# Norm roots on columns of sums, one scan for four groups, and layer norm applied on ScalarE, in a hybrid decoder step

## The chip, the cores and the metric

The kernel runs on 1 core of one Trainium2 chip. The metric is the device time of one execution in microseconds (us). The engines that matter are TensorE (PE; its weight loads are listed apart as PEld), VectorE (DVE), ScalarE (ACT), GpSimd (POOL), and SyncE (SP), whose queue issues nearly all DMA transfers. Each engine runs its own queue in order.

## The reference

One layer over 1088 tokens (1024 of a prompt, 64 of eight short continuations), width 1024: a norm, a projection into three parts of 512, an S5 state-space mixer on the first part, a chunked gating mixer on the other two, a norm on each mixer's output, an output projection, then norm, SwiGLU feed-forward and a final norm.

```python
def rmsnorm(x, g):
    r = lax.rsqrt(jnp.mean(xf * xf, axis=-1, keepdims=True) + EPS)
    return xf * r * g
def layer(x, h0r, h0i, l):
    p = rmsnorm(x, norm1[l]) @ w_in[l]
    o_s5, hr, hi = s5_mixer(p[..., :512], h0r, h0i, ...)   # complex diagonal scan, GELU, GLU
    o_cm, v_rows = chunk_mixer(p[..., 512:], ...)          # GELU, layernorm(v), tril(W_s) @ v, u * mixed
    mix = concatenate([rmsnorm(o_s5, g_s5[l]), rmsnorm(o_cm, g_cm[l])])
    x = x + mix @ w_out[l]
    return x + swiglu(rmsnorm(x, norm2[l]), w_gate[l], w_up[l], w_down[l])   # then rmsnorm(x, norm_f)
```

## The kernel before

Activations lie feature-major: 128 features on the partitions, tokens along the free axis. Tokens are taken in three chunks of 384, 384 and 320 up to the mixers' outputs (`CH`), and in four of 272 (`NH`) from the output projection on. Large products run as three single-pass matmuls on a high and a low part of each operand (`mm3`, lines 150 to 152); the parts are made by `split` (a copy on ScalarE at line 146, a subtraction on VectorE at line 147).

The stages stand in this order. **Head**, 0 to 72 us: tokens and `w_in` come in, norm1 sums squares, VectorE builds the S5 tables of powers, and TensorE makes `pu`, the S5 input; VectorE writes it to SBUF as `us`, scaled by the root `rB` (line 303). **S5 stage**, 72 to 236 us: eight passes of four groups each (`s5_a`, `s5_b`, `s5_c`) with a scan over 128 blocks, and beside them, on TensorE, the projections `pv` and `pu` of the gating mixer, its layer norm (`ln`) and its mixing (`cm_out`). **Mixers' norms, GLU (`pg`) and output projection (`po`)**, 236 to 360; **norm2 and the first operands of the feed-forward** (`x_prep`), 360 to 396; **feed-forward**, 396 to 1078; **final norm** (`finish`), 1078 to the end.

Norms need, for each token, a sum over features, which lie on partitions. `sum_sq` (line 164) multiplies a 128x128 matrix of ones with the squares, so the sum comes out on all 128 partitions at once, in PSUM as `ss`, as wide as the chunk. `rsqrt_bc` takes the root there on all of it: one activation on ScalarE (line 171), then three VectorE steps of refinement (172 to 174), each 128 x chunk. In chunk 0 of norm1 each of the eight blocks of squares goes to TensorE; in chunks 1 and 2 VectorE adds them first (`sqs`, line 195). The projection `pv` comes out token-major, so its scale must be a column: nine VectorE operations read the diagonal of `rB` into `r1c` (line 624).

The S5 pass scans four groups one after the other (line 559), each with its own decay as a constant along the row. Around each scan stand two half swaps by DMA (`Sw<-Ss`, `gw<-gt`), a correction written as `Hp`, the output matmuls `yb`, a GELU to `ys`, and a trip through DRAM (`ys_d`) to the GLU's operand `g`.

Who runs when is set at build time: the framework's scheduler sorts all instructions by a model of their times and freezes the order of each engine's queue; a few `issue_after` lines pin things. So an edit also moves instructions that it does not touch.

## Time and profile before

| | us |
|---|---|
| median of 3 runs | 1108.19 (1107.27 to 1110.16) |
| the profiled execution, whole | 1110.51 |
| its span in the trace | 1108.7 |
| PE busy | 1052.7 (95%) |
| DVE busy | 855.2 (77%) |
| ACT busy | 431.4 (39%) |
| POOL busy | 322.1 (29%) |

The shares are averages over stages that differ. In the feed-forward TensorE is busy nearly all the time and VectorE two thirds; in the head and the S5 stage both are nearly full and wait for each other. So each stage is read by itself: who is idle there, and what ended the idle time. [...]

### The profile page before, as it was taken

How to read it: one execution, taken by the hardware profiler on the slowest of the kernel's cores; microseconds unless marked ns; L12 is line 12 of the kernel's file. 1: busy time of each engine (PE TensorE's matmuls, PEld its weight loads, DVE VectorE, ACT ScalarE, POOL GpSimd, SP SyncE). 2: the span in 40 equal slices, each digit the busy share in tenths (PEclk: the TensorE clock that was granted, in tenths of full speed). 3: DMA queues.
4: the chain of work that ended last, by engine and by line, in shares of the span. 5: the costliest groups of instructions: out<-in, count | busy, mean ns of one | idle time of the engine just before them, and what ended most of it. 6: DMA issues, size and time to landing. Idle time of an engine off the chain costs nothing.

```text
span 1108.7 us, 20330 instructions
## 1 busy us (share of the span) xinstructions
PE 1052.7 (95%) x7966; PEld 1027.8 (93%) x7966; DVE 855.2 (77%) x1724; ACT 431.4 (39%) x810; POOL 322.1 (29%) x287
## 2 busy tenths in 40 slices
PE   7899999969999899999999999999998999999994
PEld 6799998869999789999999999999998999999994
DVE  7988999898988996666666666657668768757886
ACT  7314323477444443233233232232244324314561
POOL 5010350000000435425435334435333333223220
PEclk9999999989999899999999999999999999999998
DMA  8342335365233113223224223133256816514304
GB/s 278 106 139 54 95 106 150 83 193 163 97 103 107 45 57 128 74 90 131 74 74 129 85 82 128 58 109 117 69 174 223 303 39 202 185 35 150 118 16 161
DMA packets 81519, 131.19 MB, mean 118 GB/s; under 512 B 8976, under 2 KB 60048, under 8 KB 81296
## 3 DMA queue, kind: packets, MB, share of 16 engines
q1 hardware_dynamic: 81424, 129.91, 36.9%
q8 instruction: 62, 1.02, 0.4%
q14 instruction: 33, 0.27, 0.1%
HBM read 90.43 MB, written 34.24 MB: 112 GB/s over the span
## 4 chain that ended last, share of the span: by engine, by line
PE 69%; DVE 15%; DMA 8%; issue 3%; ACT 3%; POOL 1%; SPq 0%; DVEq 0%; POOLq 0%; ACTq 0%
PE u L151 12%; PE u L150 12%; PE u L152 12%; DMA h<-hid_d 4%; PE po L152 3%; PE po L151 3%; PE po L150 3%; PE ua L151 3%; PE ua L150 3%; PE ua L152 3%; PE pv L151 2%; PE pv L150 2%; PE pv L152 2%; PE ub L151 1%; PE ub L152 1%
## 5 line engine op out<-in xcount | busy, mean ns | idle before, releaser
L1052 POOL TENSOR_TENSOR tS<-q,q 128x512 f32<-128x512 f32 x22 | 29.5, 1342 | 247.0 <-DVE h L914 146.1
L150 PE MATMUL u<-xh,h 128*128 128x272 f32 x344 | 99.1, 288 | 0.0
L151 PE MATMUL u<-xl,h 128*128 128x272 f32 x344 | 99.0, 288 | 0.0
L152 PE MATMUL u<-xh,h 128*128 128x272 f32 x344 | 98.9, 288 | 0.0
L146 ACT ACTIVATE h<-q 128x512 fp32r<-128x512 f32 (+1 forms) x83 | 50.7, 614 | 81.9 <-PE u L151 59.3
L147 DVE TENSOR_TENSOR h<-q,h 128x512 fp32r<-128x512 f32 (+1 forms) x83 | 71.7, 865 | 4.1 <-ACT h L146 2.3
L150 PE MATMUL pu<-xh,cwr 128*128 128x384 f32 (+1 forms) x192 | 65.6, 346 | 6.2 <-DVE us L303 6.2
L1090 ACT ACTIVATE st<-st 128x272 f32<-128x272 f32 x88 | 37.8, 431 | 71.9 <-DVE st L1112 34.5
L152 PE MATMUL pu<-xh,cwr 128*128 128x384 f32 (+1 forms) x192 | 64.9, 341 | 0.0
L151 PEld LDWEIGHTS u<-xl,h 128*128 128x128 f32 x344 | 64.8, 189 | 0.0
L151 PE MATMUL pu<-xl,cwr 128*128 128x384 f32 (+1 forms) x192 | 64.7, 338 | 0.0
L150 PEld LDWEIGHTS u<-xh,h 128*128 128x128 f32 x344 | 64.7, 188 | 0.0
L152 PEld LDWEIGHTS u<-xh,h 128*128 128x128 f32 x344 | 64.6, 188 | 0.0
L1057 POOL TENSOR_TENSOR tS<-tS,q 128x512 f32<-128x512 f32 x22 | 30.4, 1381 | 114.7 <-DVE h L147 61.6
L146 ACT ACTIVATE fb<-q 128x512 fp32r<-128x512 f32 (+1 forms) x64 | 38.9, 609 | 57.2 <-PE u L151 38.9
L151 PE MATMUL u<-xl,fb 128*128 128x272 f32 x208 | 60.4, 290 | 0.6 <-DVE xl L147 0.6
L150 PE MATMUL u<-xh,fb 128*128 128x272 f32 x208 | 60.4, 290 | 0.0
L152 PE MATMUL u<-xh,fb 128*128 128x272 f32 x208 | 60.4, 290 | 0.0
L147 DVE TENSOR_TENSOR fb<-q,fb 128x512 fp32r<-128x512 f32 (+1 forms) x63 | 54.2, 864 | 3.7 <-ACT fb L146 2.8
L150 PE MATMUL po<-xh,cwr 128*128 128x272 f32 x192 | 56.3, 294 | 0.0
L1092 DVE TENSOR_TENSOR st<-st 128x272 f32<-128x272 f32 x88 | 54.5, 620 | 2.0
L151 PE MATMUL po<-xl,cwr 128*128 128x272 f32 x192 | 55.5, 289 | 0.0
(496 smaller groups left out, 4128.9 us busy)
## 6 DMA issues: line engine op xcount, KB each, us to landing
hid_d<-st SPq DMA_DIRECT2D x22, 952.0 KB, 4.2
...
```

The lines of the kernel that those rows point to most:

```text
L146: S.activation(hi, src, AF.Copy)
L147: return (eng or V).tensor_tensor(lo, src, hi.bitcast(F32), ALU.subtract)
L150: PE.matmul(p, wh, ah, start=start, stop=False, **kw)
L151: PE.matmul(p, wh, al, start=False, stop=False, **kw)
L152: return PE.matmul(p, wl, ah, start=False, stop=stop, **kw)
L1052: P.tensor_tensor(tS, a21, a22, ALU.add)
L1057: P.tensor_tensor(tS, tS, a11, ALU.subtract)
L1090: S.activation(dst, src, AF.Silu)
L1092: V.tensor_tensor(dst, dst, src, ALU.mult)
```

## The change

Sums of squares are made the other way round: `sum_cols` loads 128x128 squares as the weights and multiplies them with a single column of ones, so 128 tokens' sums come out as one column, 128x1, in PSUM (`cs`). A chunk has three such columns. The root is then taken on 128x3 numbers (`rsqrt_row`, tile `rcs`). TensorE spreads it: the root's column, repeated 128 times, is the weight matrix, and the identity moves, which gives the root along the free axis on all partitions (`rb`, PSUM). ScalarE copies it to SBUF, except in `finish`, where VectorE reads PSUM. The additions into `sqs` and the diagonal reads are gone; `pv`'s scale is the root's column itself. The identity is loaded ahead of the tokens.

The four scans become one over 128x512, with the decays in a table `mg` whose first column in each group is zero, so that a group starts afresh. ScalarE fills `mg` once a pass, into one buffer. Layer norm's last step goes from VectorE to ScalarE, with its bias made by a 128x1 operation on POOL.

```diff
-    def sum_sq(sq, n, p=None, first=True, last=True):
-        p = bank("ss", "sp")[:, :n] if p is None else p
-        LAST["sum"] = PE.matmul(p, ones, sq, start=first, stop=last)
+    def sum_cols(sqs, n, p=None, first=True, last=True):
+        p = bank("cs", "sp") if p is None else p
+        for i, sq in enumerate(sqs):
+            for j, (x, _) in enumerate(blocks(n)):
+                LAST["sum"] = PE.matmul(p[:, j:j + 1], sq[:, x:x + 128], ones[:, 0:1], start=first and i + j == 0,
+                                        stop=last and i == len(sqs) - 1, skip_group_check=True)
         return p
-    def rsqrt_bc(pl, p, n, scale):
+    def rsqrt_row(p, n, scale, out=None, tag="sp"):
+        r, a = (rcs[:, k, 3 * i:3 * i + len(bl)] for i in range(2))
+        LAST["rsqrt"] = S.activation(r, p, AF.Abs_reciprocal_sqrt, scale=scale, bias=epsc)
+        V.scalar_tensor_tensor(a, p, EPS / scale, r, op0=ALU.add, op1=ALU.mult)
+        V.scalar_tensor_tensor(a, a, -0.5 * scale, r, op0=ALU.mult, op1=ALU.mult)
+        V.scalar_tensor_tensor(r, a, 1.5, r, op0=ALU.add, op1=ALU.mult)
+        b = bank("rb", tag)[:, :n]
+        for j, (x, w) in enumerate(bl):
+            PE.matmul(b[:, x + 128 - w:x + 128], r[:, j:j + 1].to_broadcast([128, 128]), idn[:, 128 - w:128],
+                      start=True, stop=True)
+        if out is None:
+            return b, r
+        S.activation(out, b, AF.Copy)
+        return out, r
...
-            if c:
-                accum_sq(prep, sqs[:, :n], r[:, i, :], k == 0)
-            else:
-                N1["p"] = sum_sq(sq, n, N1.get("p"), k == 0, k == 7)
+            sq = tmp_sq(prep, n, "sq")
+            S.activation(sq, r[:, i, :], AF.Square)
+            N1[c] = sum_cols([sq], n, N1.get(c), k == 0, k == 7)
...
-        y = rsqrt_bc(prep, sum_sq(sqs[:, :n], n) if c else N1["p"], n, 1.0 / D)
-        V.tensor_copy(rB[:, n0:n0 + n], y)
+        R1[c] = rsqrt_row(N1[c], n, 1.0 / D, rB[:, n0:n0 + n], "s5")[1]
...
+        mg = mgs[pi % MG]
+        S.activation(mg[:, :, 1:128], mag8[:, gs].unsqueeze(2).to_broadcast([128, 4, 127]), AF.Copy)
...
-        V.tensor_tensor(rt, rt, Sw, ALU.add)
-        for g in range(4):
-            V.tensor_tensor_scan(gt[:, g, :], mag8[:, g0 + g:g0 + g + 1].to_broadcast([128, 128]), rt[:, g, :], 0.0,
-                                 ALU.mult, ALU.add)
+        V.tensor_tensor(Sw, rt, Sw, ALU.add)
+        V.tensor_tensor_scan(*(x.rearrange("p g c -> p (g c)") for x in (gt, mgs[pi % MG], Sw)), 0.0,
+                             ALU.mult, ALU.add)
...
-    for j in range(9):
-        V.scalar_tensor_tensor(jk, rB[:, tok(j)], 1.0, idn, op0=ALU.mult, op1=ALU.mult, accum_out=r1c[:, j:j + 1])
...
-        V.tensor_scalar(vj, vj, mv[:, j, 0:1], mv[:, j, 1:2], op0=ALU.subtract, op1=ALU.mult)
+        P.tensor_scalar(mv[:, j, 0:1], mv[:, j, 0:1], mv[:, j, 1:2], -1.0, op0=ALU.mult, op1=ALU.mult)
+        S.activation(vj, vj, AF.Identity, scale=mv[:, j, 1:2], bias=mv[:, j, 0:1])
...
-        rb = rsqrt_bc(cwp, sum_sq(sqo[:, n0:n0 + n], n), n, 1.0 / W)
+        rb, _ = rsqrt_row(sum_cols([sqo[:, n0:n0 + n]], n), n, 1.0 / W, row_tile(cwp, n))
...
-        p = sum_sq(ACC[c], NH, bank("ss", ("s5", "sp")[c % 2])[:, :NH], True, False)
-        for i in range(2):
-            sum_sq(LSQ[c, i], NH, p, False, i == 1)
+        p = sum_cols([ACC[c], LSQ[c, 0], LSQ[c, 1]], NH, bank("cs", ("s5", "sp")[c % 2]))
+        rb, _ = rsqrt_row(p, NH, 1.0 / D, None, "mm")
```

`glu_mix` and `x_prep` are edited as `cm_mix` is. Line numbers shift by 2 near the matmuls (150 becomes 152) and by about 20 further down.

The first place is TensorE's queue in the head, where norm1's sums stand among the matmuls of `pu`. Before, the sum of a whole chunk of 384 tokens (`ss`) is one matmul there:

```order
L152 MATMUL pu_567<-xh,cwr 128x320
L150 MATMUL pu_567<-xh,cwr 128x320
L151 MATMUL pu_567<-xl,cwr 128x320
L164 MATMUL ss<-sqs,ones 128x384
L152 MATMUL pu_567<-xh,cwr 128x320
L150 MATMUL pu_567<-xh,cwr 128x320
L151 MATMUL pu_567<-xl,cwr 128x320
```

After, in the same stage (`sq` are the squares, `ones` is now a single column):

```order
L152 MATMUL pu_518<-xh,cwr 128x384
L172 MATMUL cs<-ones,sq 128x1 x4
L191 MATMUL rb<-idn,rcs 128x128 x3
L172 MATMUL cs<-ones,sq 128x1 x5
L153 MATMUL pu_518<-xl,cwr 128x384
L154 MATMUL pu_518<-xh,cwr 128x384
L152 MATMUL pu_518<-xh,cwr 128x384
```

Sums now come as lots of single columns (`cs`), nine of them where one matmul stood for a whole chunk, and the spread of a root (`rb`, three matmuls) stands between them; `pu` cannot pass either.

The second place is TensorE's queue at the end of the S5 stage. Before (`yb` is the output of the last pass, `spt` the gating mixer's mixing, `ss` sums for the mixers' norms, `pg` the GLU):

```order
L585 MATMUL yb<-U,mb_833 128x136 x2
L680 MATMUL spt<-wT,v 64x128 x4
L680 MATMUL spt<-bd,v 64x64 x2
L164 MATMUL ss<-sqo,ones 128x384
L586 MATMUL yb<-Hp,QK 128x136
L585 MATMUL yb<-U,mb_833 128x136
L586 MATMUL yb<-Hp,QK 128x136 x2
L585 MATMUL yb<-U,mb_833 128x136
L586 MATMUL yb<-Hp,QK 128x136
L680 MATMUL spt<-wT,v 64x128 x4
L680 MATMUL spt<-bd,v 64x64 x2
L150 MATMUL pg<-xh,wgh 128x384 x7
```

After (`pu_2618` and `pu_2619` are the gating mixer's last projections, with 35 of their rows between the last `yb` and the first `pg`, not all shown):

```order
L609 MATMUL yb<-Hp,QK 128x136
L700 MATMUL spt<-wT,v 64x128 x6
L153 MATMUL pu_2618<-xl,cwr 128x320
L154 MATMUL pu_2618<-xh,cwr 128x320
...
L152 MATMUL pu_2619<-xh,cwr 128x320
L172 MATMUL cs<-ones,sqo 128x1 x3
...
L700 MATMUL spt<-wT,v 64x128 x4
L700 MATMUL spt<-bd,v 64x64 x2
L700 MATMUL spt<-wT,v 64x128 x4
L700 MATMUL spt<-bd,v 64x64 x2
L152 MATMUL pg<-xh,wgh 128x384 x5
```

The last pass's `yb` has moved ahead of these projections, which stood in front of it; the spread of the first mixer norm's root (`rb`) now stands 44 rows behind the first `pg`, and with it VectorE's scaling of the gating mixer's outputs (line 718 before).

The third place is VectorE's queue at the end of the kernel. Before (`x1r` and `x1a` hold the output, `rs` a root in the making):

```order
L1208 SCALAR_TENSOR_TENSOR x1r_9457<-x1r_9457,gp,rs 128x272 x2
L174 SCALAR_TENSOR_TENSOR rs<-rs 128x272
L172 SCALAR_TENSOR_TENSOR rs<-ss,rs 128x272
L1204 TENSOR_TENSOR x1r_9455<-x1r_9455,rs 128x2x272
L1204 TENSOR_TENSOR x1a<-x1a,rs 128x2x272
L1204 TENSOR_TENSOR x1r_9453<-x1r_9453,rs 128x2x272
L1208 SCALAR_TENSOR_TENSOR x1r_9457<-x1r_9457,gp,rs 128x272 x2
L173 SCALAR_TENSOR_TENSOR rs<-rs 128x272
L174 SCALAR_TENSOR_TENSOR rs<-rs 128x272
L1204 TENSOR_TENSOR x1r_9455<-x1r_9455,rs 128x2x272
```

After (`ua` is the last term of a product that is added to `x1r`, `rcs` a root on columns):

```order
L1219 TENSOR_TENSOR x1r_9563<-x1r_9563,rb 128x2x272
L1223 SCALAR_TENSOR_TENSOR x1r_9567<-x1r_9567,gp,rb 128x272 x2
L1157 TENSOR_TENSOR x1r_9567<-x1r_9567,ua 128x272
L186 SCALAR_TENSOR_TENSOR rcs<-cs,rcs 128x3
L187 SCALAR_TENSOR_TENSOR rcs<-rcs 128x3
L188 SCALAR_TENSOR_TENSOR rcs<-rcs 128x3
L186 SCALAR_TENSOR_TENSOR rcs<-cs,rcs 128x3
L187 SCALAR_TENSOR_TENSOR rcs<-rcs 128x3
L188 SCALAR_TENSOR_TENSOR rcs<-rcs 128x3
L1219 TENSOR_TENSOR x1r_9565<-x1r_9565,rb 128x2x272
```

The last addition into the output now stands behind the second of four scalings, and the last two roots, which were spread over the scalings before, stand together behind it.

## Rows read from the trace of the kernel before

**Rows 1.** Stretches: length, busy us of PE, PEld, DVE, ACT, POOL; clock; DMA share; GB/s.
```profile
30.00:72.00 42.00, 35.82 (x200) 34.48 (x198) 38.93 (x153) 10.49 (x19) 4.36 (x18) 0.92 0.27 84
...
150.00:236.00 86.00, 74.73 (x540) 65.83 (x539) 80.02 (x171) 39.42 (x81) 12.64 (x14) 0.97 0.45 129
236.00:360.00 124.00, 123.23 (x901) 122.14 (x902) 110.02 (x256) 67.11 (x136) 0.00 (x0) 0.98 0.40 128
360.00:396.00 36.00, 28.90 (x181) 26.63 (x180) 34.54 (x49) 18.44 (x28) 15.23 (x9) 0.86 0.12 38
396.00:820.00 424.00, 421.80 (x3353) 421.09 (x3353) 281.50 (x505) 130.34 (x260) 180.36 (x161) 1.00 0.31 99
```

**Rows 2.** TensorE in time, head: start us, us, engine, line, operation [idle before <-releaser].
```profile
44.81 0.33 PE L152 MATMUL pu<-xh,cwr 128*128 128x384 f32 x1
44.98 0.33 PE L150 MATMUL pu<-xh,cwr 128*128 128x384 f32 x1
...
46.08 0.81 PE L164 MATMUL ss<-sqs,ones 128*128 128x384 f32 x2
...
54.90 0.66 PE L150 MATMUL pu<-xh,cwr 128*128 128x384 f32 x1 [5.22 <-DVE us L303]
...
60.48 0.46 PE L152 MATMUL pu<-xh,cwr 128*128 128x384 f32 x1
...
67.64 0.38 PE L150 MATMUL pu<-xh,cwr 128*128 128x320 f32 x1 [0.96 <-DVE us L303]
```

**Rows 3.** A stretch of the head at the lower clock, columns as in group 1.
```profile
57.00:60.00 3.00, 3.00 (x11) 3.00 (x10) 3.00 (x16) 0.00 (x0) 0.00 (x0) 0.50 0.00 0
```

**Rows 4.** By form: count, duration ns min/median/max, first and last start; weight loads are PEld.
```profile
L164 PEld LDWEIGHTS ss<-h,ones x24: 186/189/190, 1078.1 to 1094.8; 128*128 128x128 f32 x24
...
L164 PE MATMUL ss<-sq,ones x16: 484/486/1009, 6.5 to 21.3; 128*128 128x384 f32 x16
```

**Rows 5.** By form, weight loads of 64 and 16 columns, and matmuls on the former.
```profile
L680 PEld LDWEIGHTS spt<-wT,v x128: 132/137/183, 144.1 to 229.2; 128*64 128x64 f32 x128
L680 PE MATMUL spt<-wT,v x128: 272/273/418, 144.1 to 229.3; 128*64 128x128 f32 x128
...
L517 PEld LDWEIGHTS kb<-QK,PT x64: 92/97/97, 94.2 to 210.3; 128*16 128x16 f32 x64
```

**Rows 6.** TensorE in time, end of the S5 stage, columns as in group 2.
```profile
215.72 0.88 PE L680 MATMUL spt<-wT,v 128*64 128x128 f32 x12
...
236.77 2.61 PE L150 MATMUL pg<-xh,wgh 128*128 128x384 f32 x7 [6.93 <-ACT xh L146]
```

**Rows 7.** By form, the VectorE work that the change removes or reshapes.
```profile
L195 DVE TENSOR_TENSOR sqs<-sqs,sq x14: 500/526/560, 26.8 to 58.2; 128x384 f32<-128x384 f32 x7, 128x320 f32<-128x320 f32 x7
...
L624 DVE SCALAR_TENSOR_TENSOR cwf<-rB,idn x9: 281/292/304, 33.8 to 68.5; 128x128 f32<-128x128 f32 x9
...
L559 DVE TENSOR_TENSOR_SCAN gt<-mag,Ss x32: 384/387/1464, 100.1 to 218.4; 128x128 f32<-128x128 f32 x32
...
L658 DVE TENSOR_SCALAR v<-v,mv x9: 502/528/541, 118.4 to 154.4; 128x512 f32<-128x512 f32 x9
...
L172 DVE SCALAR_TENSOR_TENSOR rsa<-ss,rsy x6: 484/550/562, 23.4 to 290.2; 128x384 f32<-128x384 f32 x4, 128x320 f32<-128x320 f32 x2
```

**Rows 8.** VectorE in time, head, a short operation.
```profile
46.11 0.21 DVE L446 TENSOR_TENSOR e<-tsb,co 128x32 f32<-128x32 f32 x1
```

**Rows 9.** VectorE in time, end of the S5 stage.
```profile
217.45 1.35 DVE L559 TENSOR_TENSOR_SCAN gt<-mag,Ss 128x128 f32<-128x128 f32 x4
...
228.47 2.20 DVE L718 SCALAR_TENSOR_TENSOR v<-v,gp,cwf 128x384 f32<-128x384 f32 x4
```

**Rows 10.** ScalarE in time, end of the S5 stage.
```profile
236.20 1.39 ACT L146 ACTIVATE xh<-g 128x384 fp32r<-128x384 f32 x4
```

**Rows 11.** VectorE in time, the last stretch.
```profile
1088.47 0.44 DVE L172 SCALAR_TENSOR_TENSOR rs<-ss,rs 128x272 f32<-128x272 f32 x1 [1.46 <-ACT rs L171]
...
1104.47 0.91 DVE L1208 SCALAR_TENSOR_TENSOR x1r<-x1r,gp,rs 128x272 f32<-128x272 f32 x2
```

More of the change, by code (lines that the diff above doesn't have):

```diff
@@ L36 @@
 GA = 1, 3
+MG = 1
 SQP = 3
@@ L113, in layer_kernel @@
     ones = cst.tile([128, 128], F32, name="ones")
+    rcs = cst.tile([128, 7, 6], F32, name="rcs")
     epsc = cst.tile([128, 1], F32, name="epsc")
@@ L159, in layer_kernel, with blocks, row_tile @@
     LAST = {}
-    def sum_sq(sq, n, p=None, first=True, last=True):
-        p = bank("ss", "sp")[:, :n] if p is None else p
-        LAST["sum"] = PE.matmul(p, ones, sq, start=first, stop=last)
-        return p
-    def rsqrt_bc(pl, p, n, scale):
-        a = pl.tile([128, NH], F32, "rsa") if isinstance(pl, Arena) and "rsa" in pl.tags else tmp_sq(pl, n, "rsa")
-        y = pl.tile([128, 384], F32, tag="rsy", name="rsy")[:, :n]
-        LAST["rsqrt"] = S.activation(y, p, AF.Abs_reciprocal_sqrt, scale=scale, bias=epsc)
-        V.scalar_tensor_tensor(a, p, EPS / scale, y, op0=ALU.add, op1=ALU.mult)
-        V.scalar_tensor_tensor(a, a, -0.5 * scale, y, op0=ALU.mult, op1=ALU.mult)
-        V.scalar_tensor_tensor(y, a, 1.5, y, op0=ALU.add, op1=ALU.mult)
-        return y
+    def blocks(n):
+        return [(x, 128) for x in range(0, n - 127, 128)] + [(n - 128, n % 128)] * (n % 128 > 0)
+    def sum_cols(sqs, n, p=None, first=True, last=True):
[4 more added lines that the diff above has]
+                                        stop=last and i == len(sqs) - 1, skip_group_check=True)
+        return p
+    cnt = {"rc": 0}
+    def rsqrt_row(p, n, scale, out=None, tag="sp"):
+        bl = blocks(n)
+        k = cnt["rc"] if cnt["rc"] < 3 else 3 + cnt["rc"] % 4
+        r, a = (rcs[:, k, 3 * i:3 * i + len(bl)] for i in range(2))
+        cnt["rc"] += 1
+        p = p[:, 0:len(bl)]
+        LAST["rsqrt"] = S.activation(r, p, AF.Abs_reciprocal_sqrt, scale=scale, bias=epsc)
[10 more added lines that the diff above has]
+        return out, r
+    def row_tile(pl, n):
+        return pl.tile([128, 384], F32, tag="rsy", name="rsy")[:, :n]
     SQT = {}
@@ L206, in layer_kernel @@
     rB = lncp.tile([128, NT], F32, name="rB")
-    r1c = lncp.tile([128, 9], F32, name="r1c")
-    sqs = prep.tile([128, 384], F32, name="sqs")
+    R1 = {}
     mhalf = lncp.tile([128, 16], F32, name="mhalf")
@@ L216, in layer_kernel @@
     Q.dma_start(gp, A["gp"])
+    Q.dma_start(idn, A["idn"])
     def pt(name, shape):
@@ L322, in layer_kernel @@
         s5_in(1, c)
-    Q.dma_start(idn, A["idn"])
     h0 = s5p.tile([128, NG, 8], F32, name="h0")
@@ L458, in layer_kernel @@
         P.memset(x, 0.0)
+    mgs = [s5w.tile([128, 4, 128], F32, name=f"mg{i}") for i in range(MG)]
+    for x in mgs:
+        V.memset(x[:, :, 0:1], 0.0)
     def part(d, pi):
@@ L466, in wt @@
         n = int(np.prod(shape))
-        t = s5w.tile([128, n], F32, tag=tag, name=name, bufs=BUFS.get(tag, 1))
+        t = s5w.tile([128, 544 if tag == "H" else n], F32, tag=tag, name=name, bufs=BUFS.get(tag, 1))[:, 0:n]
         if len(shape) == 2:
@@ L554, in s5_b @@
         V.tensor_tensor(Sw, Sw, SIf, ALU.mult)
-        V.tensor_tensor(rt, rt, Sw, ALU.add)
-        gt = wt("H", "gt", (4, 136))
-        gt = gt[:, :, 0:128]
-        for g in range(4):
-            V.tensor_tensor_scan(gt[:, g, :], mag8[:, g0 + g:g0 + g + 1].to_broadcast([128, 128]), rt[:, g, :], 0.0,
-                                 ALU.mult, ALU.add)
+        V.tensor_tensor(Sw, rt, Sw, ALU.add)
+        gt = wt("H", "gt", (4, 128))
+        V.tensor_tensor_scan(*(x.rearrange("p g c -> p (g c)") for x in (gt, mgs[pi % MG], Sw)), 0.0,
+                             ALU.mult, ALU.add)
         gw = wt("W", "gw", (4, 128))
@@ L649, in v_quarter @@
             mm3(p[:, 0:256], xh[:, k, tok(j)], xl[:, k, tok(j)], wh, wl, k == 0, k == 7)
-        S.activation(v[:, j, 256 * (q - 2):256 * (q - 1)], p[:, 0:256], AF.Gelu_apprx_tanh, scale=r1c[:, j:j + 1])
+        S.activation(v[:, j, 256 * (q - 2):256 * (q - 1)], p[:, 0:256], AF.Gelu_apprx_tanh, scale=R1[j // 3][:, j % 3:j % 3 + 1])
     def ln(j):
@@ L787, in glu_mix @@
         n0, n = CH[c]
-        rb = rsqrt_bc(gl, sum_sq(ACC5[c], n), n, 1.0 / W)
+        rb, _ = rsqrt_row(sum_cols([ACC5[c]], n), n, 1.0 / W, row_tile(gl, n))
         for m in range(4):
@@ L906, in x_prep @@
         s, half = divmod(c, 2)
-        p = sum_sq(SQX[c][0], NH, None, True, c < 3)
-        if c == 3:
-            sum_sq(SQX[c][2], NH, p, False, True)
-        rb = rsqrt_bc(fnp, p, NH, 1.0 / D)
+        p = sum_cols([x for x in SQX[c] if not isinstance(x, int)], NH)
+        rb, _ = rsqrt_row(p, NH, 1.0 / D, row_tile(fnp, NH))
         if half == 0:
@@ L1069, in prep @@
             wsplit(n, a12, kk)
-    cnt = {"u": 0, "st": 0, "hr": 0, "t": 0}
+    cnt.update(u=0, st=0, hr=0)
     def nxt(key, lst):
```

5 lines of the change are left out of this document (removed).

## The prediction

> **What bounds the kernel now.** I read the table of stretches first. From 396 us on TensorE is busy 421.8 of 424 us [rows 1] and its queue there holds the same instructions in the same order before and after, so the feed-forward, two thirds of the time, can neither gain nor lose. What can move lies before 396 us and at the very end. There VectorE carries the load: 38.9 of 42 us in the head's second half, 80.0 of 86 at the end of the S5 stage, 34.5 of 36 in norm2's stage; only from 236 to 360 us is TensorE the fuller one, 123.2 of 124 against 110.0 [rows 1].
>
> The second view is TensorE's timeline in the head, with what ended its idle time: 5.22 and 0.96 us, both ended by VectorE's `us` [rows 2]. After the 5.22 us the granted clock is 0.50, the lower level [rows 3], and the matmuls' steps grow [rows 2]. Between the starts at 54.90 and 60.48 us stand 17 steps of 0.33 us, against 0.17 from 44.81 to 44.98 at the upper level (records overlap, so a step is shorter than a record) [rows 2]. That is 17 x 0.155 = 2.6 us lost. TensorE thus loses 5.2 + 1.0 + 2.6 = 8.8 us in the head because VectorE is late.
>
> The third is the same view at the end of the S5 stage: 6.93 us of waiting at 236.77, where the GLU's first matmul waits for ScalarE's split of its operand `g` [rows 6], which itself comes off the S5 chain at 236.20 [rows 10]. TensorE has nothing left to do in that gap. The first seven matmuls behind it take 2.61 us, 0.35 a step: the lower clock again. Idle and slow steps together cost about 14 us: 86.0 - 74.7 = 11.3 in the stretch [rows 1], 0.8 after it, and some 2 at the lower clock.
>
> **The change part by part.** The sum is made against the profiled execution: 1110.51 us, of which the span is 1108.7 and 1.8 lie around it. It is 2.3 above the median of 1108.19; I carry the difference over to the median.
>
> *Price of a sum.* A sum over 384 tokens was one matmul in two records: the pair spans 0.81 us [rows 2] and one record lasts 0.484 [rows 4], so a step is 0.33 and the matmul costs 0.65. Now it is three matmuls of one moving column, each with two weight loads of 128 columns. No such matmul is in the trace. Near it: twelve `spt` records in 0.88 us, each 0.273 long [rows 6, 5], so (0.88 - 0.273) / 11 = 0.055 a step, with weights of 64 columns; such a load lasts 0.137 us, one of 16 columns 0.097, one of 128 columns 0.188 [rows 4, 5]. Lower bound of a column's matmul: 2 x 0.055 = 0.11. Upper: two loads end to end, 0.38. I take 0.22, twice the 64-column step per record: loads of 16, 64 and 128 columns lie on a line of 0.8 ns a column, so the load's columns look like what paces a short matmul. Three columns then cost 0.66, like the matmul that they replace. A spread is three matmuls of 128 moving columns, together what one sum over 384 cost: 0.65 more for each root.
>
> [...]
>
> *Head.* In norm1, chunks 1 and 2 had one sum each and chunk 0 eight; now all 24 blocks have three columns. TensorE gains 72 x 0.22 + 3 x 0.65 - 10 x 0.65 = 15.8 + 2.0 - 6.5 = 11.3 us of work. VectorE loses 14 additions of 0.53 (7.4), nine diagonal reads of 0.29 (2.6) [rows 7] and nine root steps that fall from 0.55 to about 0.21, the length of a 128x32 operation [rows 7, 8] (3.1): 13 us. It then no longer holds TensorE up, and the 8.8 us go. Net: 11.3 - 8.8 = +2.5, that is, TensorE's new work eats the waiting that it ends. Bounds: -5.5 (0.11 a column), +14 (0.38).
>
> *S5 stage.* Off VectorE: nine layer-norm steps of 0.53 [rows 7] = 4.8. Four scans take 1.35 us together [rows 9]; one over 512 is not in the trace. It saves three fixed shares; the 0.21 of a 128x32 operation [rows 8] bounds one share from above, so it takes 1.35 - 0.63 = 0.72 to 1.35. I take 1.1, nearer to the four that it replaces: 8 x 0.25 = 2. The new work lies on ScalarE and POOL, which are idle half the time or more there [rows 1]. `mg` has one buffer, so ScalarE's filling waits for the scan before and a split may queue behind it; ScalarE's slack hides that unless the passes draw closer than they do now.
>
> [...]
>
> The order moves too. The last `yb` has passed 35 `pu` rows of about 0.15 us, which now cover the trip through DRAM that left TensorE idle; and the first mixer norm's root with the scalings behind it (2.2 us at 228.47 for four [rows 9], as much again for their subtractions) stands after the first GLU matmuls. So VectorE has 6.8 + 4.4 = 11 us less ahead of `g`, and TensorE nothing to wait for. Of the 14 us lost there I take 12 back. Bounds: -5 (only the gap is covered, because the swaps by DMA pace the passes), -15 (all of it).
>
> *236 to 360 us.* TensorE is full, so its additions count: sums are equal, but six spreads at 0.65 = 3.9 and two of norm2's at about 0.45 come on top: +4.8. The half-speed steps after 236 are already counted. A spread stands in TensorE's queue in front of GLU matmuls and waits for three VectorE steps; behind it everything stops. The scheduler has placed it 44 rows behind the first GLU matmul, about 7 us at 0.17, which covers a root unless VectorE is late. The 0.8 us that it is idle there now [rows 1] take some back: +4, from +2 to +9.
>
> *Norm2's stage.* VectorE saves 6 x 0.25, TensorE's part comes in series with it: -0.5, from -2 to +2.
>
> *End.* VectorE works without a break from 1088.47 to 1105.4 [rows 11]. Twelve root steps of 0.44 fall to 0.2, some 3 us. But the last addition stands behind the second scaling, and after it squares, three columns, a root, three steps and a spread run in series, about 2.5 us in which VectorE waits. Net -0.5, from -2 to +2.
>
> Sum: +2.5 - 12 + 4 - 0.5 - 0.5 = -6.5. From 1110.5 that is 1104.0, from the median 1101.7; I say 1101.5.
>
> **The rivals.**
> *The columns are dear.* If a weight load of 128 columns does not overlap the next (0.38 us), the head costs 72 x 0.16 = 11.5 more, the mixers' and norm2's sums 30 x 0.16 = 5 more (the end's hide in idle TensorE). The sum is -6.5 + 16.5 = +10: 1118. For it speaks the 0.188 of one load, against it the 0.055 step with loads of 0.137, which overlap there. It decides from 0.28 us on, where 102 x 0.064 = 6.5 eats the gain.
> *VectorE's relief is idle.* The S5 passes are paced by swaps through DMA; then the freed time turns into waiting and the stage gives 5 instead of 12: -6.5 + 7 = +0.5, no change, 1108.5. For it: VectorE still waits some 6 us in that stretch (80.0 of 86). Against it: 93% busy is close to full.
> *The columns are cheap.* At 0.11 the head gives 8 more, the later sums 3, the S5 stage, which then starts earlier, perhaps 2: -6.5 - 13 = -19.5, 1088.5. For it: a weight load may hide behind a long matmul in front; against it: three or nine columns stand in a row, and only the first has one.
>
> **How the numbers follow.** Forecast 0.58, idle relief 0.17, dear columns 0.15, cheap ones 0.10. A measurement of this kernel tells about 0.3%, 3.3 us, from no change. The forecast and the cheap columns are faster: 0.68; idle relief is the same: 0.17; dear columns are slower: 0.15. The forecast's own range is 1095 to 1105; with the bounds of the column on both sides the range is 1087 to 1114.
>
> **What would show it.** Steps of `cs` at about 0.11 us a record; no idle time ended by `us` near 50 us and no lower clock after it; the end of `pu` in the head within 2 us of now; one scan near 1.1 us; the first GLU matmul near 225 to 228 us at the upper clock; the stretch from there to the end of the output projection some 4 us longer; the feed-forward unchanged in length. I am wrong if the head ends more than 5 us later, if `rb` rows carry waits of several us in TensorE's queue, or if VectorE's idle time in the S5 stage grows by what was taken off it.

## The result and the profile after

The changed kernel is slower by half a per cent: median 1117.62 us of 6 runs (1113.70 to 1118.48), against 1110.22 for the kernel before beside it (6 runs), ratio 1.0054 [1.0030, 1.0079]. The profiled execution took 1118.08 us, its span 1116.3, which is 7.6 above the span before. The forecast was 1101.5; even the upper end of the range, 1114, is missed.

To see where the time went I cut the span at the starts of four TensorE records: the first `pv` (end of the head), the first `pg` (GLU), the last `po` that reads `xl` (the last `po` but one), and the first `u` that uses `cwr` (feed-forward under way). Lengths in us:

| stage | before | after | change | forecast |
|---|---|---|---|---|
| head, to the first `pv` | 71.7 | 81.5 | +9.8 | +2.5 |
| S5 stage, to the first `pg` | 165.1 | 152.2 | -12.9 | -12 |
| GLU and output projection, to the last `po` | 126.2 | 131.0 | +4.8 | +4 |
| norm2's stage, to the first `u` on `cwr` | 26.9 | 31.8 | +4.9 | -0.5 |
| feed-forward and end | 718.9 | 719.8 | +0.9 | -0.5 |
| sum | 1108.7 | 1116.3 | +7.6 | -6.5 |

Three stages came as forecast. The head and norm2's stage, 7.3 and 5.4 off, make 12.7 of the 14.1 us between forecast and result.

The table of stretches of the kernel after (columns as in [rows 1]; the two stretches of 4 us have no row there):

```profile
30.00:72.00 42.00, 42.00 (x291) 42.00 (x291) 31.29 (x125) 11.63 (x24) 4.12 (x18) 1.00 0.30 91
150.00:236.00 86.00, 83.52 (x614) 76.00 (x613) 79.23 (x157) 39.45 (x87) 21.54 (x20) 1.00 0.51 140
236.00:360.00 124.00, 124.00 (x957) 124.00 (x956) 106.68 (x265) 70.31 (x144) 0.00 (x0) 1.00 0.36 119
360.00:396.00 36.00, 28.66 (x199) 26.89 (x197) 27.56 (x44) 15.85 (x26) 12.36 (x8) 0.91 0.16 53
...
18.00:22.00 4.00, 4.00 (x18) 4.00 (x17) 3.90 (x15) 2.05 (x4) 0.00 (x0) 1.00 1.06 317
26.00:30.00 4.00, 4.00 (x27) 4.00 (x27) 2.88 (x7) 4.00 (x10) 0.00 (x0) 1.00 0.33 88
...
57.00:60.00 3.00, 3.00 (x23) 3.00 (x22) 1.39 (x4) 0.44 (x1) 1.49 (x9) 1.00 0.00 0
```

From 30 to 72 us TensorE never waits now, where it was idle for 6.2 of 42 us [rows 1], and the clock at 57 us is the upper one, 1.00 against 0.50 [rows 3]: the 8.8 us that were to come back did. The head is longer all the same. Compare 18 to 22 us with 26 to 30: TensorE is full in both, but gets 18 matmul records done in the one and 27 in the other. TensorE's timeline of the start, columns as in [rows 2]:

```profile
7.16 2.72 PE L172 MATMUL cs<-ones,sq 128*128 128x1 f32 x12 [7.16 <-ACT sq L292]
9.74 0.67 PE L152 MATMUL pu<-xh,cwr 128*128 128x384 f32 x1
10.21 0.52 PE L153 MATMUL pu<-xl,cwr 128*128 128x384 f32 x1
10.53 0.52 PE L152 MATMUL pu<-xh,cwr 128*128 128x384 f32 x1
...
11.17 1.27 PE L172 MATMUL cs<-ones,sq 128*128 128x1 f32 x6
12.30 0.99 PE L154 MATMUL pu<-xh,cwr 128*128 128x384 f32 x2
...
17.89 2.55 PE L172 MATMUL cs<-ones,sq 128*128 128x1 f32 x12
20.30 0.67 PE L154 MATMUL pu<-xh,cwr 128*128 128x384 f32 x1
...
24.29 0.52 PE L154 MATMUL pu<-xh,cwr 128*128 128x384 f32 x1
24.61 0.38 PE L152 MATMUL pu<-xh,cwr 128*128 128x384 f32 x1
24.83 0.34 PE L153 MATMUL pu<-xl,cwr 128*128 128x384 f32 x1
25.00 0.34 PE L154 MATMUL pu<-xh,cwr 128*128 128x384 f32 x1
...
40.76 1.39 PE L172 MATMUL cs<-ones,sq 128*128 128x1 f32 x12
42.02 0.42 PE L153 MATMUL pu<-xl,cwr 128*128 128x384 f32 x1
```

A step of `pu` is 0.32 us up to 24.61 and 0.17 from 24.83 on; 0.33 is what [rows 2] showed where [rows 3] has the clock at 0.50. Twelve records of single columns take 2.41 us from 17.89 to the next `pu` at 20.30, and 1.26 from 40.76 to 42.02. So TensorE runs at half pace for the first 14.9 us after 9.74. In the kernel before, steps are 0.18 from 9.56 us on. The clock column, the granted clock as a share of full speed, reads 1.00 in both stretches. The first clock entry of this trace begins with the rise, at 24.7 us, and the column counts the time ahead of that entry as full clock. So at the start of a span I read the level from the steps.

The forms that the change brought (columns as in [rows 4]; they answer to [rows 4, 7]):

```profile
L172 PE MATMUL cs<-ones,sq x144: 164/250/373, 7.2 to 55.7; 128*128 128x1 f32 x144
...
L186 DVE SCALAR_TENSOR_TENSOR rcs<-cs,rcs x17: 146/154/163, 28.5 to 1105.9; 128x3 f32<-128x3 f32 x17
...
L582 DVE TENSOR_TENSOR_SCAN gt<-mg,Sw x8: 1190/1205/1225, 107.3 to 216.2; 128x512 f32<-128x512 f32 x8
```

The 144 records of `cs` are 72 matmuls of two records each, 24 matmuls to a chunk; the nine in the queue shown with the change are a part of a chunk.

Then the first `pg` and the split before it, which answer to [rows 6] and [rows 10]:

```profile
233.73 1.16 PE L152 MATMUL pg<-xh,wgh 128*128 128x384 f32 x5
```
```profile
232.66 1.79 ACT L148 ACTIVATE xh<-g 128x384 fp32r<-128x384 f32 x5
```

No idle time stands before `pg` and its five records take 1.16 us, so both halves of the S5 loss are gone.

Norm2's stage, TensorE's sums and spreads and then VectorE's root and scaling:

```profile
361.21 0.72 PE L172 MATMUL cs<-ones,cwf 128*128 128x1 f32 x6
...
365.60 0.74 PE L191 MATMUL rb<-idn,rcs 128*128 128x128 f32 x6
...
379.45 0.85 PE L191 MATMUL rb<-idn,rcs 128*128 128x128 f32 x6
```
```profile
362.94 0.16 DVE L188 SCALAR_TENSOR_TENSOR rcs<-rcs 128x3 f32<-128x3 f32 x1
...
365.17 0.44 DVE L862 TENSOR_TENSOR x1a<-x1a,po 128x272 f32<-128x272 f32 x1 [1.53 <-PE po L154]
366.81 0.91 DVE L932 SCALAR_TENSOR_TENSOR h<-x1a,gp,cwf 128x272 f32<-128x272 f32 x2 [1.20 <-ACT cwf L195]
...
375.67 1.25 DVE L188 SCALAR_TENSOR_TENSOR rcs<-rcs 128x3 f32<-128x3 f32 x1
380.19 0.69 DVE L149 TENSOR_TENSOR wa<-q,wa 128x512 fp32r<-128x512 f32 x1 [3.26 <-ACT wa L148]
380.83 0.92 DVE L932 SCALAR_TENSOR_TENSOR h<-x1a,gp,cwf 128x272 f32<-128x272 f32 x2
```

The first root is done at 363.10, but its spread starts at 365.60, 2.5 us later, behind `po` and the first `u` matmuls in TensorE's queue. The scalings start at 366.81 and, for the second root, 380.83 (before: 361.25 and 374.57). No `rb` row carries idle time: TensorE was busy with what stood in front. Not all of the delay is the spread's. VectorE's own queue holds an addition ahead of the first scaling that waits 1.53 us for `po`; the wait that ends last, 1.20 us, is the one for ScalarE's copy of `rb`. Ahead of the second scaling stands `wa`, which waits 3.26 us for ScalarE.

### The profile page after: what moved, and what is told of

Same layout as the page of the kernel before. It is cut to its first block, busy times and chain, and to the rows that moved or that the text cites. A ratio compares the mean times of both kernels' runs of the same rounds, so it can differ in the third digit from the quotient of the medians.

```text
span 1116.3 us, 20964 instructions
## 1 busy us (share of the span) xinstructions
PE 1076.9 (96%) x8284; PEld 1060.8 (95%) x8284; DVE 824.2 (74%) x1657; ACT 440.6 (39%) x839; POOL 325.6 (29%) x296
## 4 chain that ended last, share of the span: by engine, by line
PE 46%; DMA 7%; DVE 5%; POOL 2%; issue 2%; ACT 1%; DVEq 0%; SPq 0%; POOLq 0%; ACTq 0%
PE u L154 11%; PE u L153 11%; PE u L152 11%; DMA h<-hid_d 5%; PE ua L152 2%; PE ua L153 2%; PE ua L154 2%; DMA hid_d<-st 1%; PE ub L153 1%; PE ub L154 1%; PE ub L152 1%; DVE xl L149 1%; DMA q<-in_w_up_dram 1%; ACT xh L148 1%; DVE cwr L149 1%
## 5 line engine op out<-in xcount | busy, mean ns | idle before, releaser
L149 DVE TENSOR_TENSOR h<-q,h 128x512 fp32r<-128x512 f32 (+1 forms) x83 | 71.7, 864 | 4.3 <-ACT h L148 2.5
L154 PE MATMUL po<-xh,cwr 128*128 128x272 f32 x192 | 55.0, 290 | 0.0
L152 PE MATMUL po<-xh,cwr 128*128 128x272 f32 x192 | 54.6, 289 | 0.0
```

Source lines behind the costliest of these rows:

```text
L149: return (eng or V).tensor_tensor(lo, src, hi.bitcast(F32), ALU.subtract)
L152: PE.matmul(p, wh, ah, start=start, stop=False, **kw)
L154: return PE.matmul(p, wl, ah, start=False, stop=stop, **kw)
```

## The experiments

Each run's expectation is quoted as put on record before it ran. All edits are made on the changed kernel; "old" means the helpers `sum_sq` and `rsqrt_bc` for the norm named. Upper = start of the first `pu` step at the upper pace; stages as above, from each run's one profiled execution; then the span, the median (runs), and the ratio to the kernel before:

```
kernel                  upper  head    S5   GLU norm2  rest    span  median     ratio
before                    9.6  71.7 165.1 126.2  26.9 718.9  1108.7
after                    24.6  81.5 152.2 131.0  31.8 719.8  1116.3  1117.62(6)  1.0054 [1.0030,1.0079]
e1_warm                   9.5  77.3 155.4 131.2  32.2 723.2  1119.3  1121.47(10) 1.0088 [1.0058,1.0117]
e2_norm1_old             12.5  74.6 153.0 131.0  33.0 720.6  1112.2  1114.29(10) 1.0026 [1.0006,1.0045]
e3_prep_old              15.7  77.4 152.9 129.0  28.8 722.8  1111.0  1116.05(10) 1.0038 [1.0019,1.0056]
e4_final_old             25.2  81.8 152.9 131.1  31.5 720.1  1117.4  1116.28(10) 1.0041 [1.0023,1.0058]
e5_norms_old             12.2  74.2 153.6 132.6  26.5 718.3  1105.2  1107.53(10) 0.9963 [0.9950,0.9977]
e6_chunk0_old            12.4  83.2 153.7 131.0  32.3 724.2  1124.4  1125.70(4)  1.0135 [1.0107,1.0163]
e7_layernorm_old         17.0  77.7 159.1 132.3  29.8 723.4  1122.2  1124.55(4)  1.0130 [1.0107,1.0153]
e8_scan_old              24.2  81.2 159.9 132.5  32.6 720.6  1126.9  1126.38(4)  1.0139 [1.0120,1.0158]
e9_wide                  12.5  76.0 152.2 131.5  31.8 719.1  1110.6  1114.88(10) 1.0027 [1.0010,1.0044]
e10_wide_prep_old        11.8  75.6 152.7 129.5  29.6 723.6  1111.0  1113.11(10) 1.0014 [1.0002,1.0027]
e11_norms_1_2_f_old      12.7  74.7 152.8 129.0  28.3 723.2  1108.0  1108.50(10) 0.9977 [0.9962,0.9993]
e12_mixer_split          13.2  73.6 154.6 135.6  26.7 724.3  1114.8  1116.50(9)  1.0036 [1.0018,1.0055]
e13_layernorm_only       12.1  74.1 159.1 133.9  26.4 720.0  1113.5  1115.69(4)  1.0063 [1.0041,1.0084]
e14_scan_only            11.9  73.9 162.4 127.9  27.3 716.0  1107.5  1112.83(10) 1.0026 [1.0012,1.0040]
e15_norms_old_late_idn   12.0  74.0 161.3 132.4  27.6 718.4  1113.7  1116.11(6)  1.0043 [1.0027,1.0059]
e16_wide_late_idn        11.2  76.0 152.3 131.4  32.9 719.4  1112.1  1114.70(10) 1.0033 [1.0017,1.0049]
e17_three_old_late_idn    9.8  72.0 162.4 130.5  27.7 722.2  1114.8  1116.61(7)  1.0047 [1.0031,1.0063]
```

**The head: the pace of TensorE at the start.** First a warm-up on TensorE ahead of the first sums:

```diff
+    for i in range(12):
+        PE.matmul(bank("wm", "mm")[:, 0:128], ones, ones, start=True, stop=True)
```

> The changed kernel with twelve 128x128 products of the ones matrix with itself put on TensorE while it waits for the first tokens (results unused); all else as in the changed kernel. Theory A: the head is 7 us longer than forecast because TensorE starts on single-column matmuls and its steps stay at 0.32 us instead of 0.17 until 24.6 us; with long products ahead the steps are 0.17 from about 10 us on, the first pv comes at 74 to 75 us instead of 81.5, and the end comes 5 to 8 us sooner: about 1110 to 1113. Theory B (rival): the head is long because of the work of 72 columns itself; then the first pv stays at 81 to 82 and the time within 1 us.

The upper pace was there at the first `pu` steps, 0.18 us at 9.54, and was lost again, with steps of 0.32 from 9.72 on: after the first 12 records of single columns the clock column reads 0.50 from 10 to 16 us, and the upper pace is back at 16.5. The head took 77.3, 4.2 less than in the changed kernel, but the S5 stage 3.2 and the feed-forward 3.4 more, and the whole is no faster (the intervals overlap). It agrees with the pace as cause and settles nothing by itself.

Then norm1 alone with the old helpers (its sums again one matmul over 384 columns, VectorE adding squares):

```diff
-            sq = tmp_sq(prep, n, "sq")
-            S.activation(sq, r[:, i, :], AF.Square)
-            N1[c] = sum_cols([sq], n, N1.get(c), k == 0, k == 7)
+            if c:
+                accum_sq(prep, sqs[:, :n], r[:, i, :], k == 0)
+            else:
+                sq = tmp_sq(prep, n, "sq")
+                S.activation(sq, r[:, i, :], AF.Square)
+                N1["p"] = sum_sq(sq, n, N1.get("p"), k == 0, k == 7)
...
```

> The changed kernel with norm1 alone as before (sums by the ones matrix, additions into sqs, root 128 wide, diagonal reads). Both theories: the first pv returns to 71 to 73 us. What differs is what is kept: if the S5 stage's gain of 13 us is its own (layer norm, scan, order), the first pg comes at 224 to 227 and the end at 1106 to 1109; if that gain is only slack that the late head left for VectorE to catch up, the first pg stays near 232 and the end near 1114 to 1116.

Upper pace at 12.5, head 74.6: 6.9 of the 9.8 us come back. It undoes the column's price as well as the pace, so the next run changes only the number of columns that move:

```diff
-                LAST["sum"] = PE.matmul(p[:, j:j + 1], sq[:, x:x + 128], ones[:, 0:1], start=first and i + j == 0,
+                LAST["sum"] = PE.matmul(p[:, 128 * j:128 * j + 128], sq[:, x:x + 128], ones, start=first and i + j == 0,
-        p = p[:, 0:len(bl)]
+        p = p[:, 0:128 * len(bl):128]
```

> The changed kernel with 128 columns of ones moving through each block's weights instead of one (same weight loads, same count; the root reads every 128th column). By the forms of the spread, 128 moving columns take 0.11 us a record, the same as a single column's 0.104, so TensorE's time for the sums stays within 1 us. Theory A: the clock stays low in the head because single-column matmuls leave TensorE nearly empty although it counts as busy; then steps of 0.17 come from 9 to 13 us on as before the change, the first pv at 74 to 76, and the time falls by 3 to 6 us. Theory B (rival): it is the weight loads or the short matmuls' number that does it; then the lower steps last to 15 to 25 us again and the first pv stays at 77 to 82.

TensorE at the start of this kernel:

```profile
11.08 1.38 PE L172 MATMUL cs<-ones,sq 128*128 128x128 f32 x6
12.22 0.60 PE L154 MATMUL pu<-xh,cwr 128*128 128x384 f32 x2
12.65 0.34 PE L152 MATMUL pu<-xh,cwr 128*128 128x384 f32 x1
12.83 0.33 PE L153 MATMUL pu<-xl,cwr 128*128 128x384 f32 x1
```

The same number of matmuls and loads, computing each sum 128 times over, is faster: the upper pace comes at 12.5 instead of 24.6, and the head ends 5.5 us earlier. The span falls by 5.7; the median is 1.0027 of before, with an interval that overlaps that of the changed kernel, so the stage carries the verdict. This is the decisive run: work, loads and VectorE's part are equal, TensorE's queue holds the same records up to 15.8 us, past the rise, and only what TensorE moves has changed. e10 and e16, which also move 128 columns, have the rise at 11.8 and 11.2.

What the pace costs shows without any edit of the head. The changed kernel, e3, e4, e7 and e8 have one and the same order of records on TensorE up to the first `pv`. Where the upper pace comes at 15.7 and 17.0 us (e3, e7) the head takes 77.4 and 77.7, where it comes at 24.2 to 25.2 it takes 81.2 to 81.8. From the changed kernel to e3 that is 24.6 - 15.7 = 8.9 us less of half pace; with steps of 0.32 against 0.174 they are worth 8.9 x 0.146 / 0.32 = 4.1, and the head is 4.1 shorter. TensorE's rise in e3:

```profile
15.12 0.78 PE L152 MATMUL pu<-xh,cwr 128*128 128x384 f32 x2
15.74 0.34 PE L153 MATMUL pu<-xl,cwr 128*128 128x384 f32 x1
```

A third run: chunk 0 of norm1 old, chunks 1 and 2 on columns (with three diagonal reads for chunk 0's scales).

```diff
-            N1[c] = sum_cols([sq], n, N1.get(c), k == 0, k == 7)
+            N1[c] = (sum_cols([sq], n, N1.get(c), k == 0, k == 7) if c else
+                     sum_sq(sq, n, N1.get(c), k == 0, k == 7))
...
```

> The changed kernel with norm1's first chunk alone in the old form: eight sums by the ones matrix (5.2 us of TensorE against 5.0 for 24 columns), a root 128 wide, three diagonal reads. Theory A: it is the columns among the first matmuls that keep the steps at 0.32 us until 15 to 25 us; then the steps are 0.17 from 9 to 13 us on, the first pv comes at 74 to 77 instead of 77 to 81.5, and the time falls by 3 to 6 us. Theory B (rival): TensorE's work in the head is the same, so the first pv and the time stay within 1 us of the changed kernel.

The start is cured (12.4), but the head takes 83.2, the longest of all. TensorE's timeline and three stretches of this kernel show why:

```profile
38.97 3.41 PE L172 MATMUL cs<-ones,sq 128*128 128x1 f32 x18
42.93 4.00 PE L172 MATMUL cs<-ones,sq 128*128 128x1 f32 x18 [0.55 <-DVE rcs L202]
48.21 5.12 PE L172 MATMUL cs<-ones,sq 128*128 128x1 f32 x24
53.19 0.67 PE L152 MATMUL pu<-xh,cwr 128*128 128x384 f32 x1
```
```profile
40.00:42.00 2.00, 2.00 (x11) 2.00 (x11) 2.00 (x14) 1.25 (x4) 0.00 (x0) 0.50 0.00 0
46.00:48.00 2.00, 2.00 (x11) 2.00 (x10) 2.00 (x16) 0.94 (x2) 0.00 (x0) 0.50 0.01 4
50.00:52.00 2.00, 2.00 (x11) 2.00 (x11) 2.00 (x9) 0.52 (x2) 0.00 (x0) 0.50 0.02 4
```

Here the scheduler has put 18, 18 and 24 single-column records in a row. TensorE counts as 2.00 of 2.00 us busy, and the granted clock is 0.50, the lower level, in all three stretches. Here the column does show it: the clock fell while the engine was busy, at 39.4 us, 0.4 us into the first of these rows and behind 18 single-column records that stand among `pu` steps from 35.9 us on, and it rose again at 56.5 (means of 0.85 over 38 to 40 us and 0.88 over 56 to 58).

**Norm2's stage: the spread in TensorE's queue.** `x_prep` alone old, first on the changed kernel, then on e9:

```diff
-        p = sum_cols([x for x in SQX[c] if not isinstance(x, int)], NH)
-        rb, _ = rsqrt_row(p, NH, 1.0 / D, row_tile(fnp, NH))
+        p = sum_sq(SQX[c][0], NH, None, True, c < 3)
...
+        rb = rsqrt_bc(fnp, p, NH, 1.0 / D)
```

> The changed kernel with norm2's roots alone as before. Theory A: the 5 us lost between 360 and 396 us are the spread's place in TensorE's queue: the root is done on VectorE and then waits 2.5 us behind output products, and at the second root behind slow steps; with the old form the first u<-ex comes 4 to 5 us sooner (375.5 to 376.5 against 380.5) and the end 3 to 5 us sooner. Theory B (rival): the loss is the lower clock behind an idle stretch, which is there in both forms; then under 1 us is gained.

> The kernel with 128 moving columns, and norm2's roots as before. If the head's clock (4 to 6 us) and the spread's wait in norm2's stage (3 us) are separate losses, they add up: 1108 to 1111, about the time before the change. If they are not, it stays within 1 us of the kernel with 128 columns alone.

The stage falls from 31.8 to 28.8, and from 31.8 to 29.6: 3.0 and 2.2 of the 4.9 us. VectorE in e3, the last step of the first root and the scaling behind it:

```profile
358.56 0.44 DVE L189 SCALAR_TENSOR_TENSOR cwf<-cwf 128x272 f32<-128x272 f32 x1
359.04 0.92 DVE L950 SCALAR_TENSOR_TENSOR h<-x1a,gp,cwf 128x272 f32<-128x272 f32 x2
```

With the root wide, the scaling starts 0.04 us after the end of its last step; with the spread it started 3.7 us after it (363.10 to 366.81). In e3 the addition that waits for `po` stands behind the scalings, not ahead of them, so the form of the root and the order that comes with it are tested together. The feed-forward of these runs is longer (722.8 and 723.6), so the medians move by 1.6 and 1.8 only, within overlapping intervals, and e10 stays short of the 1108 to 1111 it was to reach. About half of the 4.9 goes with norm2's column form; the rest went only in runs in which more norms were old (26.5 in e5).

**The end.** The final norm alone old (`sum_sq` and `rsqrt_bc` for `p` and `rb` in `finish`):

> The changed kernel with the final norm alone as before. Theory A: the 36 columns (7.5 us of TensorE) and the spreads stand among the last products, and the last root is made in series behind the last addition; with the old form the last VectorE work ends 2 to 3 us sooner relative to the feed-forward's end, the total falls by 2 to 3 us. Theory B (rival): the end is late only because all before it is late; then the total stays within 1 us.

Rest 720.1 against 719.8, median within the intervals: the spread at the end costs nothing that can be seen. The end is late because all before it is.

**The S5 stage: which edit earned it.** All norms old, so that only the layer norm on ScalarE and the one scan remain:

> The changed kernel with all norms as before (sums by the ones matrix, roots 128 wide), so that of the change only the layer norm on ScalarE, the single scan and the early load of the identity are left. Theory A: the S5 stage's gain (first pv to first pg 152 us against 165) is VectorE's relief by layer norm and scan, and each other stage's loss comes from the norms; then first pv to first pg stays at 152 to 156, the GLU and output projection take 126 again instead of 131, and the total is 1096 to 1101. Theory B (rival): the gain comes from the order that the late column root allows, with projections as a cover; then the stage is back at 160 to 165 and the total at 1105 to 1110.

This is the lowest time of the study, 0.9963 [0.9950, 0.9977], 1105.2 us of span, though short of the 1096 to 1101 expected: the GLU and output projection take 132.6, not 126. The S5 stage keeps 153.6 without any norm on columns. Then one of the two at a time, in the changed kernel (e7, e8) and with all norms old (e13 keeps the layer norm, e14 the scan):

```diff
-        P.tensor_scalar(mv[:, j, 0:1], mv[:, j, 0:1], mv[:, j, 1:2], -1.0, op0=ALU.mult, op1=ALU.mult)
-        S.activation(vj, vj, AF.Identity, scale=mv[:, j, 1:2], bias=mv[:, j, 0:1])
+        V.tensor_scalar(vj, vj, mv[:, j, 0:1], mv[:, j, 1:2], op0=ALU.subtract, op1=ALU.mult)
```
```diff
-        V.tensor_tensor_scan(*(x.rearrange("p g c -> p (g c)") for x in (gt, mgs[pi % MG], Sw)), 0.0,
-                             ALU.mult, ALU.add)
+        for g in range(4):
+            V.tensor_tensor_scan(gt[:, g, :], mag8[:, g0 + g:g0 + g + 1].to_broadcast([128, 128]), Sw[:, g, :], 0.0,
+                                 ALU.mult, ALU.add)
```

> The changed kernel with the layer norm's last step back on VectorE (nine steps of 0.53 us). Theory A: VectorE sets the pace of the S5 stage, so first pv to first pg grows from 152 to 156 to 158 and the time by 4 to 6 us. Theory B (rival): swaps through DMA set the pace and VectorE has room, so it stays at 152 to 153.

> The changed kernel with four scans of 128 instead of one of 512, and no decay table. Theory A: one scan takes about 1.1 us and saves 0.25 a pass, so first pv to first pg grows by 1 to 3 us, to 153 to 155. Theory B (rival): the scan's elements cost what a plain operation's do, 0.55 to 0.7 us, and the stage grows by 5 to 6. Theory C: VectorE has room there, nothing changes.

> The kernel before with the layer norm's last step on ScalarE alone (and the identity loaded early). Theory A: VectorE's relief sets the S5 stage; first pv to first pg falls by its 4.8 us, from 165 to 158 to 161. Theory B (rival): the order that comes with the edit decides; then the stage falls as far as with layer norm and scan together (152 to 154) or not at all (163 to 167).

> The kernel before with the single scan of four groups alone (and the identity loaded early). One scan took 1.20 us against 1.35 for four, so VectorE is relieved by 1.2 us in all. Theory A: the S5 stage falls by 1 to 2 us, from 165 to 163 to 164. Theory B (rival): the order that comes with the edit decides; then it falls by 5 us or more, or grows.

From 165.1, the layer norm alone gives 6.0, the scan alone 2.7, both 11.5 (e5). All three also have the identity's early load and the addition ahead of the scan written to `Sw`, which no run takes apart from them in this stage; what the load does to it stands under the identity below. As whole kernels neither alone is faster than before (1.0063 and 1.0026); together they are. Taking one back from the changed kernel costs 6.9 (layer norm) and 7.7 (scan). Layer norm's 4.8 us of VectorE work came out as 6.0 and 6.9. The scan's VectorE work is only 8 x (1.35 - 1.205) = 1.2 us, so most of the 7.7 must come from elsewhere, by my guess from the order that the scheduler made around it. VectorE's waits for the swap behind the scan, after and then e8 (us in total, times, longest):

```profile
DVE gt L599 <- DMA gw<-gt: 5.7, 6, 3.0
```
```profile
DVE gt L595 <- DMA gw<-gt: 9.1, 5, 3.5
```

That is 3.4 us more. On TensorE, which waits 7.5 us in this stage in e8 against 2.5 in the changed kernel, most of the difference is one wait; in e7 (waits of 5.2) it is another:

```profile
184.32 0.97 PE L604 MATMUL yb<-U,mb 128*128 128x136 f32 x4 [3.39 <-DMA mb<-mb]
```
```profile
233.83 1.01 PE L191 MATMUL rb<-idn,rcs 128*128 128x128 f32 x6 [3.91 <-DVE rcs L188]
```

In e8 it is for the transfer of `mb`, and the clock is at 0.50 for the 3.4 us behind it (`pu` steps over 320 columns of 0.27 us up to 187.88, of 0.15 from 188.10 on). In e7 a spread stands in TensorE's queue ahead of `pg` and waits for a late root on VectorE.

**Combinations.** Norm1, norm2 and the final norm old, the two mixers' norms on columns (e11); then the gating mixer's norm old as well, so that only that of the S5 mixer stays on columns (e12):

> Norm1, norm2 and the final norm as before; the two mixers' norms, layer norm and the scan as changed. Theory A: the three places where columns cost are taken away, the S5 stage's 152 us are kept: first pv 72 to 75, first pg 225 to 228, output projection 129 to 131 us behind it, norm2's stage 27 to 29; total 1103 to 1108. Rival: VectorE, loaded again, gives the S5 stage's gain back: first pg at 232 or later and 1110 or more.

> As the kernel before it in this series, with the gating mixer's norm as before too, so that only the S5 mixer's norm is on columns. The kernel with all norms old lost 10 us in the output projection, where VectorE had a backlog of scalings. Theory A: the roots on VectorE in that stage (1.4 us each, three of each mixer) are what made the backlog; with one mixer's roots on columns the loss halves, and the total is 1101 to 1105. Rival: the backlog is the scalings that the order defers, whichever form the roots have; then the total is that of all norms old, 1105 to 1109.

e11 beats the kernel before too, 0.9977 [0.9962, 0.9993]. e12 was to be better than both and missed: its GLU stage takes 135.6, and its feed-forward 724.3. In e5 that stage holds 6.4 us more than before, 4.5 of it one wait of TensorE for VectorE:

```profile
PE po L152 <- DVE x1q L888: 4.5, 1, 4.5
```

Which mixer norm causes such a backlog is not settled: e12's split didn't show it.

**The identity's load.** It stands ahead of the tokens in all kernels above. Three runs move its one line, `Q.dma_start(idn, A["idn"])`, back to its old place (e15, on e5; e17, on e11) or behind the first tokens (e16, on e9):

> All norms as before, layer norm and scan as changed, and the identity loaded where it was before. In four kernels with norm1 as before but the identity ahead of the tokens the first pv came at 73.9 to 74.6 us, against 71.7 before. Theory A: that load, one issue of 0.46 us ahead of the first tokens, delays the start and the clock's rise; then the first pv is back at 71.5 to 72.5 and the time is 2 us under that of all norms old: 1104 to 1107. Theory B (rival): the order of the head decides; then it stays at 74.

> The changed kernel with 128 columns of ones, and the identity loaded behind the first chunk's tokens. Theory A: the start comes 0.5 us sooner and the first pv falls from 76.0 to 74 to 75.5, the time by 0.5 to 2 us. Theory B (rival): nothing in the head waits for that load, 76.0 stays.

> Norm1, norm2 and the final norm as before, the mixers' norms, layer norm and scan as changed, the identity loaded where it was before. Theory A: as the kernel with these norms old and the early load, 2 us sooner: 1105 to 1107. Theory B (rival): no gain from the later load: 1107 to 1110.

Heads of 74.0, 76.0 and 72.0 against 74.2, 76.0 and 74.7 with the early load. TensorE starts at 6.9, 6.4 and 6.5 us in these, and between 7.0 and 7.4 with the load first, so it costs 0.4, 0.7 and 0.9 us there; only in e17 did the head follow. In e15 and e17 the S5 stage grew to 161.3 and 162.4, from 153.6 and 152.8: one moved load cost more than it gave. The S5 stage of the kernel before, of e5 and of e15 (columns as in [rows 1]):

```profile
71.69:236.77 165.08, 153.04 (x1160) 141.09 (x1158) 151.46 (x336) 67.46 (x148) 28.69 (x29) 0.98 0.41 115
```
```profile
74.22:227.79 153.57, 149.72 (x1158) 139.53 (x1157) 136.48 (x281) 69.66 (x153) 33.19 (x38) 1.00 0.45 121
```
```profile
74.04:235.31 161.27, 153.11 (x1158) 142.51 (x1156) 137.82 (x285) 72.88 (x155) 34.13 (x38) 0.98 0.44 117
```

VectorE is relieved by 15.0 us in e5 and 13.6 in e15, nearly alike, but the stage gives 11.5 in the one and 3.8 in the other: in e15, 9.8 of the 13.6 turn into idle time of VectorE, and TensorE waits 8.2 us against 3.9 in e5 (before: 12.0), 3.1 of them in front of `pg`. So in these kernels the relief paid only in the order in which TensorE waited less. Whether the early load would shorten this stage in the kernel before, by itself, was not run.

## Why the prediction was wrong

**The step that failed** is the head's sum, "11.3 - 8.8 = +2.5". Its terms held. A column costs (1.39 - 0.25) / 11 = 0.104 us a record, 0.207 a matmul, against 0.22 taken, at the upper level: neither the dear nor the cheap rival. The waiting of 8.8 us went too. What the sum left out is that the new work would change TensorE's pace. I took every price at the upper level; but TensorE, starting on single columns, stays at half pace for 14.9 us. A `pu` step there is 0.32 instead of 0.174, so 14.9 x 0.146 / 0.32 = 6.8 us are lost. With the column at 0.207 the new work is 14.9 + 2.0 - 6.5 = 10.4, so 10.4 - 8.8 + 6.8 = 8.4, and 0.6 for the later start (7.16 against 6.52) make 9.0 of the 9.8 measured; e9 and e3 bear out the term of the pace. I had used the lower level as a thing that follows idle time, as in [rows 2, 3], and never asked which matmuls stand in a row.

**The second step** is norm2's, "-0.5, from -2 to +2": +4.9. I priced VectorE's steps and the spreads' time on TensorE, but not that a spread stands behind whatever the queue holds. In the GLU I had weighed that very thing and found 44 rows that cover a root; in `x_prep` such rows stand between a finished root and its spread, and VectorE waits: 1.20 us at the first root by the trace, and 3.0 or 2.2 us of the stage go with the old form and its order (e3, e10). What makes the rest of the 5.4 is open. My own sign for it, waits of several us on `rb` rows, was badly chosen: the rows show none.

**What was right.** The S5 stage, -12 forecast, -12.9 measured: the layer norm is off VectorE and the gap before `pg` is covered, as said. That the two make up 12 is in part luck: the relief of VectorE, which I counted as gained, is mostly idle in the order of e15, as the rival of that name has it (whether swaps through DMA pace the passes there is not shown). The scan's part was mis-sized: 0.15 us saved a pass, not 0.25. One scan over 512 elements takes 1.205 us, against 1.35 for four of 128 [rows 9] and 0.53 for a plain operation of 128x512 [rows 7]. The first `pg` came at 233.73 instead of 225 to 228 only because the head ended later. From there to the last `po` it was +4.8 against +4. At the end VectorE waits 1.89 and 0.45 us for the last root where 2.5 was said, and the feed-forward kept its length within 1 us.

**The rivals.** The result lies at the dear columns' 1118, but by luck and not by its mechanism: 0.38 us as a price at the upper level is refuted. At half pace a column's matmul does cost 0.40 (2.41 us for 12 records), but then `pu` is as slow. None of my rivals held the pace of TensorE.

**Open:** why the upper pace comes at 15.7 or 17.0 us in e3 and e7 and at 24 to 25 in the changed kernel, e4 and e8, whose head queues hold the same order (each trace is one execution, so the head's +9.8 is that of an execution with a late rise); why the kernels with the old norm1 reach it at 12 to 13 us, some 3 us later than before (only e17 is back at 9.8, and at a head of 72.0); and the shifts of several us in stages that an edit doesn't touch, which could not be taken apart into order, waits and clock.
